# A chunked scan on one core: the solve of its 16x16 blocks on POOL, the scaling of its state on ACT

## The chip, the core and the metric

The kernel runs on one core of one Trainium2 chip. A core has five engines that each take their own queue of instructions in order: PE (matmuls), DVE (VectorE), ACT (ScalarE), POOL (GpSimd) and SP, which here only issues DMAs. They wait for each other through semaphores. The metric is the device time of one execution in microseconds (us), lower is better.

## The reference, cut to what matters

The program is two transformer blocks, one after the other. The first has two layers with a convolution branch and a recurrent branch, the second attention, retention and a mixture of experts. The change touches the recurrence of the first block alone. For each of 8 heads and both directions it is a state of 64x64 that every token updates:

```python
def step(s, inp):
    r_t, k_t, v_t, w_t, kk_t, b_t = inp
    sa = -jnp.einsum("bhvk,bhk->bhv", s, kk_t)
    s = (s * w_t[:, :, None, :] + sa[..., None] * b_t[:, :, None, :]
         + v_t[..., None] * k_t[:, :, None, :])
    y = jnp.einsum("bhvk,bhk->bhv", s, r_t) if emit else None
    return s, y
```

It runs over 256 context tokens and then, from the state they leave, over 512 tokens, forwards and backwards, in each of two layers. Around it stand projections (w_in, w_out, the feed-forward weights), norms and the convolution.

## The kernel before, in words

The scan works in chunks of 64 tokens. Within a chunk the recurrence becomes matrix products and the inverse of a triangular 64x64 matrix; across chunks only the state M (128 partitions, two heads of 64, by 64) is carried.

One call of `scan` is one layer. It has 12 steps: 4 pairs of heads times 3 groups of 256 tokens, and each step takes both directions side by side, four chunks each. Per step:

- `decay` (L843 and on) makes the decays of the group: two matmuls `pz` (L849), tanh and exponentials on ACT, a running sum on DVE (L866). POOL clears four columns of its tile tA first (L860).
- `products` makes the scaled keys on DVE (L886 to L892) and the products `pg` on PE (L904), which DVE masks into GM (L908, or L911 where no output is wanted). `PC` holds the decay up to the end of each chunk.
- `solve` inverts the 16x16 blocks on the diagonal. The blocks lie across partitions in the wrong way, so GM's part is stored to the DRAM tile `nsc` (four stores, L682), loaded back as `NB`, 64 blocks on 64 partitions (L684), solved there, stored to `xsc` (L694), and loaded as X and its transpose by `solved` (four loads, L702). NB has one buffer. The solve itself is a loop over k from 1 to 14 with one product (L689) and one sum (L690) per k, of k(15-k) elements per partition, each of which needs the result of the one before, and one write of ones to the diagonal (L693).
- `inverse` puts the blocks together to 64x64: transposes on DVE (L948, L978), matmuls `py` and `pw` on PE (L954, L963, L984, L993), copies on ACT (L957, L987, L1001) and DVE.
- `chunks` then goes through four chunks, each a chain: psR on PE (L1021, L1024), rg on DVE (L1027), psS on PE (L1031), Z on ACT (L1033), psM on PE (L1039), and the new M on DVE (L1044). L1043 multiplies the old M by PC beforehand, for L1044 to add. Outputs `pyo` (L1051, L1054) are collected beside it.

`scan` interleaves them: while the chunks of step s run, `to_come` brings the inverse of step s+1 and the products, the solve and the decays of later steps, and `others` brings what is left of the convolution (taps on DVE, L533, in steps 0 to 5), modulation weights (matmuls `pada`, layer 0) and the output norms. Before step 0 there is a run-up in which the decays and products of the first three steps, the first two solves and the first inverse are made.

The order of each engine's queue isn't the order of the code. A list scheduler places the traced instructions by their dependences and its own estimates of how long each takes; so a change of engine moves other instructions too. In each queue the result is then taken strictly in order.

Of the kernel before, what the change touches and what calls it, by code (L numbers as in the profile page):

```python
# [16 lines left out]
AF = mybir.ActivationFunctionType  # L17
OP = mybir.AluOpType
# [110 lines left out]
def tile_two_blocks(ctx: ExitStack, tc: tile.TileContext, I: dict, out: bass.AP, dump=None, stop=None):  # L129
    nc = tc.nc  # L130
# [24 lines left out]
    def mmps(shape=None, name="mm"):  # L155
        return bank("mm", shape, name)
# [25 lines left out]
    ones = const.tile([128, 128], F32, name="ones")  # L182
# [491 lines left out]
    def solve(s, T, gs):  # L674

        for q, (d, _) in zip(T, gs):
            src = q["NT"]
            if d:
                src = wk.tile([128, 4, 64], F32, name="Nt", tag="ar", bufs=1)
                nc.vector.transpose(src, q["NT"])  # L680
            for h in range(2):
                nc.sync.dma_start(own(NSC[s % 2], d, h), src[HR[h]])  # L682
        NB = wk.tile([64, 16, 16], F32, name="NB", tag="nb", bufs=1)
        nc.sync.dma_start(NB, blocks(NSC[s % 2]))  # L684
        yield
        for k in range(1, 15):
            t = wk.tile([64, 64], F32, name="nbt", tag="nbt", bufs=1)[:, 0:k * (15 - k)].rearrange("p (a b) -> p a b", a=k)
            sh = [64, k, 15 - k]
            nc.vector.tensor_tensor(t, NB[:, 0:k, k:k + 1].to_broadcast(sh), NB[:, k:k + 1, k + 1:16].to_broadcast(sh), op=OP.mult)  # L689
            nc.vector.tensor_tensor(NB[:, 0:k, k + 1:16], NB[:, 0:k, k + 1:16], t, op=OP.add)  # L690
            if k % 2:
                yield
        nc.vector.tensor_scalar(NB.rearrange("p a b -> p (a b)")[:, 0:256:17], ones[0:64, 0:16], 1.0, None, op0=OP.mult)  # L693
        nc.sync.dma_start(blocks(XSC[s % 2]), NB)  # L694
        yield

# [312 lines left out]
    def chunks(l, S, pr, gs, T, state, emit, final, get):  # L1009
# [4 lines left out]
        def chunk(q, d, n):  # L1014
            po = py[:, d] if emit else None
            c = n if d == 0 else 3 - n
            KR, GM, Z, BT, XI, PC = (q[k] for k in ("KR", "GM", "Z", "BT", "XI", "PC"))
            M = state[d]
            pr_ = bank("sm", None, "psR")
            for h in range(2):  # L1020
                nc.tensor.matmul(pr_[HR[h], 0:64], lhsT=GM[HR[h], 0, c, 0], rhs=Z[0][HR[h], c], start=True, stop=M is None)  # L1021
            for h in range(2):
                if M is not None:
                    nc.tensor.matmul(pr_[HR[h], 0:64], lhsT=KR[HR[h], 0, CS_[c]], rhs=M[HR[h], 0], start=False, stop=True)  # L1024
            yield
            rg = wk.tile([128, 64], F32, name="rg", tag="rg", bufs=2)
            nc.vector.tensor_scalar(rg, pr_[:, 0:64], -1.0, None, op0=OP.mult)  # L1027
            yield
            ps_ = bank("sm", None, "psS")
            for h in range(2):  # L1030
                nc.tensor.matmul(ps_[HR[h], 0:64], lhsT=XI[HR[h], c], rhs=rg[HR[h]], start=True, stop=True)  # L1031
            yield
            nc.scalar.activation(Z[1][:, c], ps_[:, 0:64], AF.Copy)  # L1033
            yield
            if not (final and n == 3):
                pm = bank("sm", None, "psM")
                for i in range(2):
                    for h in range(2):
                        nc.tensor.matmul(pm[HR[h], 0:64], lhsT=BT[HR[h], c, i], rhs=Z[i][HR[h], c], start=i == 0, stop=i == 1)  # L1039
                yield  # L1040
                Mn = get("Mn").rearrange("p (a v) -> p a v", a=2)
                if M is not None:
                    nc.gpsimd.tensor_scalar(M[:, 1], M[:, 0], PC[:, c:c + 1], None, op0=OP.mult)  # L1043
                    nc.vector.scalar_tensor_tensor(Mn[:, 0], pm[:, 0:64], PC[:, c:c + 1], M[:, 1], op0=OP.mult, op1=OP.add)  # L1044
                else:
                    nc.vector.tensor_scalar(Mn[:, 0], pm[:, 0:64], PC[:, c:c + 1], None, op0=OP.mult)
                state[d] = Mn
            if emit:
                if M is not None:
                    for h in range(2):  # L1050
                        nc.tensor.matmul(po[HR[h], c], lhsT=M[HR[h], 0], rhs=KR[HR[h], 1, CS_[c]], start=True, stop=False)  # L1051
                for i in range(2):
                    for h in range(2):
                        nc.tensor.matmul(po[HR[h], c], lhsT=Z[i][HR[h], c], rhs=GM[HR[h], i, c, 1], start=M is None and i == 0, stop=i == 1)  # L1054

        for n in range(4):
            yield from abreast(chunk(q, d, n) for q, (d, g) in zip(T, gs))
# [300 lines left out]
    for t in range(6):  # L1358
        p = bank("pre", None, "rvt")
# [63 lines left out]
    for t in range(4):  # L1423
        for a, n in SEG:
            p = bank("pre", None, "pq")
# [8 lines left out]
    p = bank("w", None, "ppe")  # L1434
# [9 lines left out]
    for t in range(6):  # L1444
        r = LAT[:, 4 + t:5 + t]
        for i in range(2):
            p = bank("pre", None, "pkv")
# [19 lines left out]
    for t in range(6):  # L1467
        rk = SS[:, 4 + t]
        k, kp = KTL[t], KP[:, t:t + 1]
# [241 lines left out]
    for t in range(4):  # L1711
        xr = XR[t // 2][:, t % 2]
        for c in range(2):
            p = mmps(name="prow")
# [502 lines left out]
```

## Time and profile before

| | |
|---|---|
| median of 3 runs | 4015.07 us (4010.14 to 4015.51) |
| profiled execution | 4013.53 us, span 4011.7 us |
| PE, DVE, ACT, POOL busy over the span | 94%, 68%, 42%, 8% |
| scan of layer 0, run-up and steps 0 to 10 | 300 to 676 us |
| scan of layer 1, run-up and steps 0 to 10 | 1525 to 1857 us |

A span is the time from the first to the last instruction. An engine is busy while it has an instruction under way; matmuls are pipelined, so a busy PE isn't PE at its peak. In the rows below a form such as `64x14 f32<-64x14 f32` reads partitions by elements, output from input, and "idle before us" is idle time of the engine just before the group, with what ended it.

### The profile page before, as it was taken

Reading aid. Unit: us, or ns where it says so; the run is one execution under the profiler, and the core shown is the slowest. Engines: PE = TensorE matmul, PEld = TensorE weight load, DVE = VectorE, ACT = ScalarE, POOL = GpSimd, SP = SyncE. Lnnn points to the kernel's source line nnn. Section 1 sums busy time; section 2 is a strip of 40 time slices with the busy share of each in tenths; the row PEclk is TensorE's granted clock in tenths of the full one; section 3 lists DMA queues with packets and bytes.
Section 4 is the critical chain, followed back from the end, with each engine's and each line's share of the span. In section 5 each row is a group of like instructions: output and inputs, shape, how many; then the busy total and the mean of one; then the engine's idle time right before and its main releaser. Section 6 shows DMA issues by size and latency. Waiting matters only on the chain. (4 is left out here: it accounts for less than half of the span.)

```text
span 4011.7 us, 69029 instructions
## 1 busy us (share of the span) xinstructions
PE 3774.9 (94%) x27579; PEld 2827.9 (70%) x27579; DVE 2731.7 (68%) x5439; ACT 1695.0 (42%) x2530; POOL 333.9 (8%) x349
## 2 busy tenths in 40 slices
PE   6998999999999998999999998996999999999997
PEld 4787777888888786776787786675565777664443
DVE  4779865843433778876744545657877899987776
ACT  3233342321212334452322334544655677666555
POOL 0001111000000001110000000001101122122111
PEclk7999999999999998899999998997999999999999
DMA  6122323332322321124445421035979899998996
GB/s 204 47 79 69 115 71 98 117 123 84 126 84 85 100 72 25 32 45 125 152 151 153 106 74 42 1 117 198 360 279 351 306 363 363 371 354 331 374 368 240
DMA packets 353911, 677.75 MB, mean 169 GB/s; under 512 B 118759, under 2 KB 230194, under 8 KB 323474
## 3 DMA queue, kind: packets, MB, share of 16 engines
q1 hardware_dynamic: 343024, 636.89, 45.3%
q0 software_dynamic: 9312, 34.56, 3.4%
q8 instruction: 218, 3.57, 0.4%
q10 hardware_dynamic: 1250, 1.85, 0.1%
q14 instruction: 107, 0.88, 0.1%
HBM read 635.33 MB, written 37.90 MB: 168 GB/s over the span
## 5 line engine op out<-in xcount | busy, mean ns | idle before, releaser
L431 ACT ACTIVATE wh<-wst 128x1024 fp32r<-128x1024 f32 (+2 forms) x222 | 222.7, 1004 | 990.7 <-PE pc L441 513.1
L1830 DVE TENSOR_TENSOR ml<-E,mh 128x2048 fp32r<-128x2048 f32 x236 | 536.2, 2286 | 91.5 <-PE pu L1878 44.3
L1829 ACT ACTIVATE mh<-E 128x2048 fp32r<-128x2048 f32 x236 | 447.6, 1916 | 185.9 <-PE pu L1878 146.8
L441 PE MATMUL px<-Hh,wl 128*128 128x512 f32 (+2 forms) x1216 | 487.8, 402 | 13.8 <-DVE wl L432 13.8
L441 PE MATMUL px<-Hh,wh 128*128 128x512 f32 (+3 forms) x1216 | 486.1, 401 | 13.3 <-ACT wh L431 7.1
L441 PE MATMUL px<-Hl,wh 128*128 128x512 f32 (+3 forms) x1216 | 485.5, 400 | 0.6 <-DVE Hl L419 0.6
L432 DVE TENSOR_TENSOR wl<-wst,wh 128x1024 fp32r<-128x1024 f32 (+2 forms) x222 | 255.4, 1151 | 270.6 <-ACT wh L431 268.4
L1878 PE MATMUL pu<-ml,ch 128*64 128x512 f32 (+2 forms) x968 | 272.3, 399 | 22.4 <-DVE ml L1830 22.2
L1878 PE MATMUL pu<-mh,ch 128*128 128x512 f32 (+1 forms) x968 | 279.3, 403 | 6.9 <-DVE ch L1866 4.2
L441 PEld LDWEIGHTS px<-Hh,wh 128*128 128x128 f32 (+1 forms) x1216 | 232.2, 191 | 72.6 <-ACT wh L431 9.4
L441 PEld LDWEIGHTS px<-Hh,wl 128*128 128x128 f32 (+1 forms) x1216 | 231.8, 191 | 72.8 <-DVE wl L432 18.7
L441 PEld LDWEIGHTS px<-Hl,wh 128*128 128x128 f32 (+1 forms) x1216 | 232.4, 191 | 55.6 <-DVE Hl L419 3.5
L533 DVE SCALAR_TENSOR_TENSOR acc<-ZC,VT,acc 128x272 f32<-128x272 f32 (+2 forms) x600 | 253.0, 477 | 2.5 <-ACT acc L528 2.5
L1878 PEld LDWEIGHTS pu<-mh,ch 128*128 128x128 f32 (+1 forms) x968 | 171.8, 184 | 86.5 <-issue 25.0
L1830 DVE TENSOR_TENSOR ml<-st,mh 128x2048 fp32r<-128x2048 f32 x86 | 196.0, 2286 | 42.8 <-PE pu L1878 24.5
L1878 PEld LDWEIGHTS pu<-ml,ch 128*64 128x64 f32 (+2 forms) x968 | 149.4, 159 | 92.0 <-DVE ml L1830 34.1
L441 PE MATMUL pc<-Hh,wh 128*128 128x256 f32 x672 | 193.0, 288 | 1.0 <-ACT Hh L418 0.9
L441 PE MATMUL pc<-Hl,wh 128*128 128x256 f32 x672 | 191.9, 286 | 0.5 <-DVE Hl L419 0.5
L441 PE MATMUL pc<-Hh,wl 128*128 128x256 f32 (+1 forms) x672 | 190.3, 284 | 0.1
L1829 ACT ACTIVATE mh<-st 128x2048 fp32r<-128x2048 f32 x86 | 163.2, 1917 | 55.3 <-PE pu L1878 31.7
L315 DVE SCALAR_TENSOR_TENSOR as<-adt,CS,as 128x512 f32<-128x512 f32 x224 | 161.3, 747 | 36.4 <-DMA adt<-in_w_ada_dram 20.4
L1134 DVE SCALAR_TENSOR_TENSOR XT<-px,MOD,XT 128x512 f32<-128x512 f32 x66 | 49.4, 749 | 188.0 <-PE px L441 187.7
(602 smaller groups left out, 7864.2 us busy)
## 6 DMA issues: line engine op xcount, KB each, us to landing
E<-in_w_mlp_dram SPq DMA_DIRECT2D x288, 1024.0 KB
st<-in_w_mlp_dram SPq DMA_DIRECT2D x94, 1024.0 KB
wst<-in_w_in_dram SPq DMA_DIRECT2D x29, 1024.0 KB
adt<-in_ada_w_dram SPq DMA_DIRECT2D x96, 256.0 KB
adt<-in_w_ada_dram SPq DMA_DIRECT2D x96, 256.0 KB
wst<-in_ffn_wg_dram SPq DMA_DIRECT2D x22, 1024.0 KB
wst<-in_ffn_wu_dram SPq DMA_DIRECT2D x22, 1024.0 KB
adaw<-in_ada_w_dram SPq DMA_DIRECT2D x16, 1024.0 KB
```

Source lines behind the costliest of these rows:

```text
L315: nc.vector.scalar_tensor_tensor(acc[s], t, c, acc[s], op0=OP.mult, op1=OP.add)
L431: nc.scalar.activation(wh, t[:, :, c0:c0 + n], AF.Copy)
L432: nc.vector.tensor_tensor(wl, t[:, :, c0:c0 + n], f32(wh), op=OP.subtract)
L441: nc.tensor.matmul(p[0:m, 0:n], lhsT=wa[:, k, 0:m], rhs=ha[:, k, a:a + n], start=k == 0 and first, stop=k == nk - 1 and last)
L533: nc.vector.scalar_tensor_tensor(o, z[:, j + a:j + a + n], cw(j), o, op0=OP.mult, op1=OP.add)
L1134: nc.vector.scalar_tensor_tensor(o, src, gate, o, op0=OP.mult, op1=OP.add)
L1829: nc.scalar.activation(wh, t, AF.Copy)
L1830: nc.vector.tensor_tensor(wl, t, f32(wh), op=OP.subtract)
L1878: nc.tensor.matmul(p[0:xa.shape[2]], lhsT=xa[:, kt], rhs=w[part][:, c:c + 512], start=kt == 0 and j == 0, stop=last and j == len(parts) - 1)
```

## The change

Two edits. The solve's products, sums and its write of the diagonal are issued on POOL (`nc.gpsimd`) in place of DVE. The scaling of M by the decay up to the end of the chunk, which stood on POOL, becomes an ACT copy with a scale per partition.

```diff
         for k in range(1, 15):
...
-            nc.vector.tensor_tensor(t, NB[:, 0:k, k:k + 1].to_broadcast(sh), NB[:, k:k + 1, k + 1:16].to_broadcast(sh), op=OP.mult)
-            nc.vector.tensor_tensor(NB[:, 0:k, k + 1:16], NB[:, 0:k, k + 1:16], t, op=OP.add)
+            nc.gpsimd.tensor_tensor(t, NB[:, 0:k, k:k + 1].to_broadcast(sh), NB[:, k:k + 1, k + 1:16].to_broadcast(sh), op=OP.mult)
+            nc.gpsimd.tensor_tensor(NB[:, 0:k, k + 1:16], NB[:, 0:k, k + 1:16], t, op=OP.add)
             if k % 2:
                 yield
-        nc.vector.tensor_scalar(NB.rearrange("p a b -> p (a b)")[:, 0:256:17], ones[0:64, 0:16], 1.0, None, op0=OP.mult)
+        nc.gpsimd.tensor_scalar(NB.rearrange("p a b -> p (a b)")[:, 0:256:17], ones[0:64, 0:16], 1.0, None, op0=OP.mult)
...
                 if M is not None:
-                    nc.gpsimd.tensor_scalar(M[:, 1], M[:, 0], PC[:, c:c + 1], None, op0=OP.mult)
+                    nc.scalar.activation(M[:, 1], M[:, 0], AF.Copy, scale=PC[:, c:c + 1])
                     nc.vector.scalar_tensor_tensor(Mn[:, 0], pm[:, 0:64], PC[:, c:c + 1], M[:, 1], op0=OP.mult, op1=OP.add)
```

The scheduler then orders all queues anew. Three places show it. In the names, `nsc_258` and `nsc_259` (`xsc_260` and `xsc_261`) are the two DRAM tiles, used in turn by even and odd steps; `XT`, `scanbuf` are the large tiles from which the scan cuts its buffers.

SP, the DMA queue, in the first steps of layer 1's scan, before:

```order
L684 DMA NB<-nsc_259 64x16x16
L682 DMA nsc_258<-scanbuf_14542 64x4x64 x2
L682 DMA nsc_258<-Nt 64x4x64 x2
L694 DMA xsc_261<-NB 64x16x16
L702 DMA XT<-xsc_261 64x4x64 x4
L684 DMA NB<-nsc_258 64x16x16
```

The same place in the change:

```order
L684 DMA NB<-nsc_259 64x16x16
L694 DMA xsc_261<-NB 64x16x16
L702 DMA XT<-xsc_261 64x4x64 x4
L682 DMA nsc_258<-scanbuf_14542 64x4x64 x2
L682 DMA nsc_258<-Nt 64x4x64 x2
L684 DMA NB<-nsc_258 64x16x16
```

The stores of the next step's blocks to nsc, which stood between the load of NB and the store of its result, now stand behind the loads of that result.

PE, layer 1, where the inverse for step 3 stands, before:

```order
L1021 MATMUL psR<-scanbuf_14543,scanbuf_14542 64x64 x4
L954 MATMUL py<-XT,scanbuf_14542 64x64 x16
L963 MATMUL pw<-XT 64x64 x16
L904 MATMUL pg<-scanbuf_14543,XT 64x128 x9
L984 MATMUL py<-XT,scanbuf_14542 64x32 x16
L904 MATMUL pg<-scanbuf_14543,XT 64x128
L993 MATMUL pw<-XT 32x32 x16
L924 MATMUL pt<-CF,XT 64x64 x32
```

And in the change:

```order
L1031 MATMUL psS<-rg,XT 64x64 x2
L1051 MATMUL pyo<-scanbuf_14543,XT 64x64
L904 MATMUL pg<-scanbuf_14543,XT 64x128 x7
L954 MATMUL py<-XT,scanbuf_14542 64x64 x16
L904 MATMUL pg<-scanbuf_14543,XT 64x128 x9
L1031 MATMUL psS<-rg,XT 64x64 x2
L963 MATMUL pw<-XT 64x64 x16
L1039 MATMUL psM<-scanbuf_14543 64x64 x8
```

The inverse stood in one piece between the last chunk of step 2 and the first of step 3; now its first matmuls stand among the second chunk of step 2, beside the products pg of step 4.

POOL, the run-up of layer 0 (an ISA row sets the engine up for the operation behind it), before:

```order
L652 MEMSET scanbuf_2187 128x1032
L860 MEMSET tA 128x4 x6
L1043 ISA
L1043 TENSOR_SCALAR XT<-XT,PC 128x64 x8
L860 MEMSET tA 128x4 x2
```

And in the change:

```order
L652 MEMSET scanbuf_2187 128x1032
L860 MEMSET tA 128x4 x2
L689 ISA
L689 TENSOR_TENSOR nbt<-NB 64x14
L693 TENSOR_SCALAR NB<-ones 64x16
L690 TENSOR_TENSOR NB<-NB,nbt 64x14
L860 MEMSET tA 128x4
L689 TENSOR_TENSOR nbt<-NB 64x26
```

The solve has taken the place of the scaling of M, and the clearing of tA for the decays stands among its operations.

## Rows read from the trace of the kernel before

**Rows 1.** The page's first part: busy us, share of the span, instructions.

```profile
PE 3774.9 (94%) x27579; PEld 2827.9 (70%) x27579; DVE 2731.7 (68%) x5439; ACT 1695.0 (42%) x2530; POOL 333.9 (8%) x349
```

**Rows 2.** Busy time by stage: stretch, its length, busy us (instructions), clock, DMA share, GB/s.

```profile
core 0: us, PE busy (x) PEld busy (x) DVE busy (x) ACT busy (x) POOL busy (x), PEclk, DMA share, GB/s
300.00:345.00 45.00, 34.84 (x536) 28.78 (x532) 43.00 (x138) 20.11 (x49) 0.42 (x4) 0.84 0.16 30
345.00:527.00 182.00, 172.34 (x3328) 134.21 (x3330) 149.00 (x556) 73.52 (x192) 26.48 (x53) 0.97 0.40 116
527.00:676.00 149.00, 140.60 (x2644) 111.04 (x2646) 100.73 (x369) 54.94 (x144) 19.31 (x45) 0.98 0.22 53
1525.00:1568.00 43.00, 33.39 (x539) 27.02 (x539) 34.69 (x119) 20.67 (x50) 0.62 (x6) 0.83 0.17 31
1568.00:1727.00 159.00, 147.46 (x2997) 123.45 (x2999) 130.11 (x501) 72.64 (x191) 25.69 (x54) 0.88 0.16 32
1727.00:1857.00 130.00, 120.68 (x2347) 93.42 (x2344) 87.47 (x330) 49.42 (x136) 18.34 (x42) 0.96 0.24 56
```

**Rows 3.** The solve's products and sums: count, ns min/median/max, first and last start.

```profile
L689 DVE TENSOR_TENSOR nbt<-NB x336: 123/190/264, 313.3 to 1836.1; 64x14 f32<-64x14 f32 x24, 64x36 f32<-64x36 f32 x24, 64x50 f32<-64x50 f32 x24, 64x56 f32<-64x56 f32 x24
...
L690 DVE TENSOR_TENSOR NB<-NB,nbt x336: 134/187/271, 313.5 to 1836.3; 64x14 f32<-64x14 f32 x24, 64x36 f32<-64x36 f32 x24, 64x50 f32<-64x50 f32 x24, 64x56 f32<-64x56 f32 x24
```

**Rows 4.** Timeline of SP's queue, start of layer 1's scan: start us, us, issue.

```profile
1555.19 0.57 SPq L684 DMA_DIRECT2D NB<-nsc  x1
1555.81 1.34 SPq L682 DMA_DIRECT2D nsc<-scanbuf  x2
1557.19 1.27 SPq L682 DMA_DIRECT2D nsc<-Nt  x2
1570.23 0.57 SPq L694 DMA_DIRECT2D xsc<-NB  x1
1574.18 2.58 SPq L702 DMA_DIRECT2D XT<-xsc  x4
1576.87 0.57 SPq L684 DMA_DIRECT2D NB<-nsc  x1
```

**Rows 5.** The same queue in the run-up of layer 0's scan.

```profile
306.31 1.24 SPq L682 DMA_DIRECT2D nsc<-Nt  x2
309.19 0.60 SPq L684 DMA_DIRECT2D NB<-nsc  x1
...
328.21 0.57 SPq L694 DMA_DIRECT2D xsc<-NB  x1
```

**Rows 6.** M's scaling on POOL: all; then layer 0's steps 0-5, 6-10.

```profile
L1043 POOL TENSOR_SCALAR XT<-XT,PC x160: 434/446/2484, 347.3 to 1864.2; 128x64 f32<-128x64 f32 x160
...
L1043 POOL TENSOR_SCALAR XT<-XT,PC 128x64 f32<-128x64 f32 x40 | 24.4, 618 | 124.7 <-DVE XT L1044 61.2 <-DVE NB L690 57.1 <-DVE nbt L689 6.2
...
L1043 POOL TENSOR_SCALAR XT<-XT,PC 128x64 f32<-128x64 f32 x36 | 16.5, 468 | 97.6 <-DVE XT L1044 71.7 <-DVE nbt L689 11.6 <-DVE XT L1046 10.1
```

**Rows 7.** Timeline of POOL from 465.3 to 469.2 us.

```profile
466.17 3.04 POOL L1043 TENSOR_SCALAR XT<-XT,PC 128x64 f32<-128x64 f32 x2 [13.03 <-DVE NB L690]
```

**Rows 8.** Timeline of DVE in the same stretch, two of 18 rows.

```profile
466.40 0.41 DVE L886 TENSOR_TENSOR scanbuf<-zz,tB 128x256 f32<-128x256 f32 x1
466.73 0.18 DVE L690 TENSOR_TENSOR NB<-NB,nbt 64x36 f32<-64x36 f32 x1
```

**Rows 9.** Other operations on POOL: ns min/median/max, starts; second, a sum of two inputs.

```profile
L173 POOL CAST CM<-cmf x1: 292/292/292, 5.7 to 5.7; 128x128 int8<-128x128 f32 x1
...
L1791 POOL TENSOR_TENSOR hr<-hr,AS x8: 1257/1378/3041, 2730.9 to 2748.5; 128x512 f32<-128x512 f32 x8
L1791 POOLq EVENT_SEMAPHORE  x7: 17/43/43, 2730.3 to 2743.8; - x7
```

**Rows 10.** ACT by line and shape, 345 to 527 us: busy us, mean ns, idle before.

```profile
L1033 ACT ACTIVATE scanbuf<-psS 128x64 f32<-128x64 f32 x48 | 9.4, 224 | 37.2 <-PE psS L1031 37.2
...
L885 ACT ACTIVATE tA<-tA,KC,VT 128x256 f32<-128x256 f32 x10 | 6.0, 596 | 3.2 <-DVE tA L866 3.2
```

## The prediction

> **What bounds the kernel now.** I read the page's busy table first, then busy time by stage, then the rounds of the solve on the DMA queue. Over the whole span PE is busy 94% of the time and DVE 68% [rows 1], but the edit touches the two scans alone, and there the picture is another one. Six stages matter [rows 2]: for layer 0 the run-up (300 to 345 us), steps 0 to 5 (345 to 527) and steps 6 to 10 (527 to 676), for layer 1 the run-up (1525 to 1568), steps 0 to 5 (1568 to 1727) and steps 6 to 10 (1727 to 1857). In the four stages with steps PE lacks work for 9.7, 8.4, 11.5 and 9.3 us, 38.9 us in all: that is all that any relief of DVE could give back there. A step lasts 182/6 = 30.3 us, 149/5 = 29.8, 159/6 = 26.5 and 130/5 = 26.0 us.
>
> Beside PE runs a second thing that repeats in every step, the round of the solve. The queue of SP loads NB, waits for the solve, stores it to xsc, loads X from there, and only then loads the next NB, since NB has one buffer. In layer 1 this reads: NB issued at 1555.19, store at 1570.23, loads of X from 1574.18, next NB at 1576.87 [rows 4], a round of 21.7 us, of which 15.0 lie between load and store and 6.7 after it. The store of the next step's blocks to nsc (1555.81 to 1558.46) lies inside the round, under the solve, and costs it nothing. A round of 21.7 us fits into a step of 26 us.
>
> **The change, part by part.** *DVE loses the solve*: 336 products (L689) and 336 sums (L690) of 0.19 us each [rows 3], some 127 us of records over 24 solves. DVE is busy 149 of 182 us in layer 0's steps 0 to 5 [rows 2]; its queue gets shorter, and whatever PE waits for from DVE comes earlier. The gain lies between nothing (PE has enough to do anyway) and the 38.9 us of PE's idle time. Where the round, below, sets the step, nothing is gained, and that is layer 1's steps 0 to 5; of the other three stages (27.4 us idle) I take about half, since ACT and DMA end waits of PE too: **-13 us**.
>
> *POOL gets the solve.* No row of before shows a two-input operation of 14 to 56 elements on POOL. The nearest are these. A one-input conversion of 128 elements takes 0.292 us and a two-input one of 512 elements 1.257 us at least [rows 9]. The 28 operations have 40 elements on average (the sum of k(15-k) over 14 values of k is 560), so they read 80, fewer than the 128 of the first row; an estimate a little under it is 0.27 us. The scaling of M, with 64 elements and a scalar per partition, took 0.446 us in the median [rows 6]. Each of the 28 waits for the one before it; handling a wait took 0.04 us on this queue [rows 9]. So one operation costs between 0.31 and 0.49 us; I take 0.38, nearer to the low end, since the solve's operations have no scalar operand but broadcast and strided ones.
>
> To that comes the port. The same scaling of M took 0.618 us on average in layer 0's steps 0 to 5 and 0.468 in steps 6 to 10, against its median of 0.446 and a worst case of 2.484 us [rows 6]. The worst one shows why: the pair at 466.17 us needed 3.04 us [rows 7] while DVE ran one operation with two inputs in SBUF after the other, at their usual 0.18 and 0.41 us [rows 8]. POOL stood still and DVE did not. [...] So I add 0.17 us per operation in steps 0 to 5, where the convolution's taps run on DVE, and 0.02 later (0.618 and 0.468 less 0.446): a solve of 28 x 0.55 + 0.4 = 15.8 us early and 28 x 0.40 + 0.4 = 11.6 us late, the 0.4 for the diagonal. [...]
>
> *The queue of SP is written in another order.* Behind the run-up, the order of the changed program has the stores to nsc of the next step after the loads of X, not before the store to xsc. They come out of the solve's shadow into the round: 2.6 us to issue [rows 4] and 1.6 us from the last store to the NB load that needs it (307.55 to 309.19, [rows 5]). From the NB load to the first product are 4.1 us (309.19 in [rows 5], 313.3 in [rows 3]). The round is then 4.1 + solve + 6.7 + 2.6 + 1.6 = **15.0 us + solve**: 30.8 us early, 26.6 late. Layer 0: 30.8 against steps of 30.3 is 0.5 x 6 = 3 us, and late 26.6 against 29.8 nothing. Layer 1: 30.8 against 26.5 is 4.3 x 6 = 26 us, and late 26.6 against 26.0, for four steps that have a solve, 2 us. Sum: **+31 us**. Queued behind the waiting xsc store on SP are those nsc stores, the loads of X and layer 0's ada weights; PE waits for them at L954.
>
> *PE's order follows suit.* Counted over the order, 1.34 steps of psS matmuls lie between a step's last pg and its first py in before (mean of steps 3 to 11 of both layers), 0.91 in the change. PE takes its queue in order, so at L954 it stands where the round is late. This is the place at which the 31 us are paid; it isn't counted twice.
>
> *The run-up.* The first solve took 19.0 us from load to store (309.19 to 328.21, [rows 5]); on POOL 4.1 + 15.8 = 19.9, and more if the taps hold the port, in both layers. Bounds 0 and 16 us (twice the 7.8 us by which a starved solve, below, is longer); I take **+4**.
>
> *M's scaling goes to ACT*: 160 operations. A copy of 64 elements from PSUM took 0.224 us there, one of 256 elements from SBUF with two operands per partition 0.596 [rows 10]; I take 0.35, 56 us in all on an engine busy 73.5 of 182 us [rows 2]. The scaled M is wanted only after psR, rg, psS, Z and psM of the next chunk, which hides it; behind it in ACT's queue wait the copies of Z and py. Bounds 0 and 56 us, taken **+2**; without that move it would have stood behind the solve on POOL.
>
> Sum: -13 + 31 + 4 + 2 = **+24 us** on the profiled execution's 4013.5 us (4011.7 us of span and 1.8 around it). That run lies 1.5 us under the median of the runs, so the forecast in terms of the median is 4039 us.
>
> **The rivals.** *Faster*: POOL is quick enough. At 0.31 us and no port waits a solve takes 9.1 us, the round 24.1 us, under every stage's step; the 31 us vanish and DVE's relief stays, up to 36 us of the 38.9: 3980 at best, about 3992 as a middle. It decides at a round of 26.5 us, a solve of 11.5 us or 0.40 us per operation with its waits. For it speaks that POOL is empty in the scans; against it the 0.618 us of early scalings. *Nothing to measure*: the round just fits, and PE's own work hides the rest: 4015. *Starved*: at 0.49 us and twice the port wait early solves take 28 x 0.83 + 0.4 = 23.6 us, late ones 15.2; rounds of 38.6 and 30.2 cost 50 + 73 + 2 + 17 = 142 us and the run-up 16: 4170 at the end, 4110 as a middle. For it speaks the one 2.48 us row, against it that such rows are few: the median is 0.446.
>
> **How the numbers follow.** The forecast (8 to 60 us slower) 0.42; faster 0.30; no difference 0.16; starved 0.12. A difference of 0.2%, 8 us, is about what a measurement of this kernel can tell from none. Slower is 0.54, same 0.16, faster 0.30. The range leaves out the far half of the starved case and the tail of the faster one: 3980 to 4100, reaching over the low bound of POOL's cost to much of the high one.
>
> **What would show it.** L689 and L690 on POOL with spacings near 0.4 us late and 0.55 early; 15 to 16 us from first product to diagonal in early steps; nsc stores on SP behind the loads of X; steps of layer 1's first half near 30 us, with PE idle before py at L954; layer 0's second half a little shorter. If the spacing is under 0.40 us early too, or steps of layer 1 don't grow although the round does, the forecast is wrong; if solves take over 20 us, it is too low.

## The result, and the profile after

The change makes the kernel slower: 4122.1 us (median of 4 runs, 4108.9 to 4127.3) against 4015.3 us for the kernel before on the same chip (4 runs, 4010.1 to 4018.5), a ratio of 1.027 with a 95% interval of 1.0245 to 1.0295. That is 107 us more, where the forecast had 24 and the range ended at 4100. The direction was right, the size was not, and neither was the mechanism, as the rows show.

First the page's busy table of the kernel after (its span is 4106.9 us), to be held against [rows 1]:

```profile
PE 3781.5 (92%) x27579; PEld 2846.9 (69%) x27579; DVE 2660.9 (65%) x4743; ACT 1738.0 (42%) x2689; POOL 468.5 (11%) x885
```

DVE has lost 696 instructions and 71 us of busy time (2731.7 less 2660.9), POOL has gained 135, ACT 43. The work has moved as the diff says, and no engine is near its limit through it. The stages, cut at the same events as in [rows 2] (the stages with steps run from the first Z of a scan to that of its step 6 and on to that of its step 11), columns as there:

```profile
300.00:342.00 42.00, 26.94 (x474) 23.75 (x471) 32.20 (x80) 15.05 (x37) 16.19 (x51) 0.77 0.15 25
342.00:556.00 214.00, 181.05 (x3417) 143.93 (x3414) 141.89 (x400) 91.00 (x244) 61.31 (x197) 0.92 0.35 100
556.00:722.00 166.00, 143.43 (x2616) 114.20 (x2616) 84.33 (x232) 64.41 (x179) 38.44 (x128) 0.93 0.20 48
1570.00:1612.00 42.00, 29.59 (x484) 24.89 (x486) 21.29 (x54) 15.39 (x38) 14.76 (x54) 0.69 0.15 26
1612.00:1793.00 181.00, 145.42 (x3012) 123.67 (x3008) 115.84 (x327) 78.91 (x229) 60.63 (x193) 0.88 0.15 29
1793.00:1956.00 163.00, 130.23 (x2384) 104.52 (x2384) 77.71 (x220) 66.53 (x184) 37.20 (x127) 0.84 0.18 44
```

The four stages with steps now last 214 + 166 + 181 + 163 = 724 us, against 182 + 149 + 159 + 130 = 620 in [rows 2]: 104 us, the whole loss (the two profiled spans differ by 95 us). PE lacks work in them for 33.0 + 22.6 + 35.6 + 32.8 = 124 us, against 38.9. So 85 of the 104 us are new idle time of PE. The other 19 are PE being busy longer with about the same matmuls (11429 records against 11316): its granted clock is 0.92, 0.93, 0.88 and 0.84 in place of 0.97, 0.98, 0.88 and 0.96. Each of these values is a mean of time at the full clock (1.0) and time at half of it (0.5), the only two values in both traces; the matmuls of pyo (L1054) average 219 ns at the one and 311 at the other in the kernel after. The run-ups are no longer than before: the first Z comes at 342.1 us against 345.5 in layer 0, and in layer 1 890 us after the first Z of layer 0's last step, against 892.

What PE waits for, from the table of waits of the kernel before, and then of the kernel after (us in total, times, longest):

```profile
PE py L954 <- DVE XT L948: 7.6, 7, 2.4
```

```profile
PE py L954 <- DVE XT L948: 98.0, 18, 10.4
```

This one wait, the first matmul of the inverse for the transposed X, has grown by 90 us. Two of the 18 waits, 20 us, lie in the run-ups, which did not become longer; the other 16, 78 us, lie in the 22 steps, in all four stages (14.4, 11.9, 28.1 and 23.4 us). They make up most of the 85 us. It is not POOL that is slow. The solve's operations on POOL, grouped by line (count, busy us and mean ns, idle before):

```profile
L690 POOL TENSOR_TENSOR NB<-NB,nbt 64x14 f32<-64x14 f32 (+6 forms) x336 | 107.8, 321 | 24.3
L689 POOL TENSOR_TENSOR nbt<-NB 64x14 f32<-64x14 f32 (+6 forms) x336 | 106.9, 318 | 350.9 <-DMA NB<-nsc 326.6
```

POOL idles for the load of NB, and for nothing else of note. From the first product to the last operation a solve takes 11.3 us on average (9.4 to 12.9 over 24 solves, worked out from their starts and ends), where DVE had needed 13.3 with other work in between. The solve has become shorter, and X comes later. How, the queues show around one step of layer 1. First SP, to be held against [rows 4]:

```profile
1657.07 0.59 SPq L684 DMA_DIRECT2D NB<-nsc  x1
1672.41 0.57 SPq L694 DMA_DIRECT2D xsc<-NB  x1
1674.96 2.61 SPq L702 DMA_DIRECT2D XT<-xsc  x4
1677.61 1.27 SPq L682 DMA_DIRECT2D nsc<-scanbuf  x2
1683.55 1.24 SPq L682 DMA_DIRECT2D nsc<-Nt  x2
1686.51 0.59 SPq L684 DMA_DIRECT2D NB<-nsc  x1
```

Then PE in the same stretch (in brackets the idle time before an instruction and what ended it):

```profile
1672.96 1.08 PE L904 MATMUL pg<-scanbuf,XT 64*64 64x128 f32 x14
1678.62 1.97 PE L954 MATMUL py<-XT,scanbuf 64*64 64x64 f32 x32 [4.57 <-DVE XT L948]
1680.38 1.51 PE L904 MATMUL pg<-scanbuf,XT 64*64 64x128 f32 x16
```

And DVE:

```profile
1678.12 0.45 DVE L948 STREAM_TRANSPOSE XT<-XT 128x256 f32<-128x256 f32 x1 [4.49 <-DMA XT<-xsc]
...
1681.06 0.69 DVE L908 TENSOR_TENSOR scanbuf<-pg,CB 128x512 f32<-128x512 f32 x1 [0.85 <-PE pg L904]
...
1682.15 0.69 DVE L908 TENSOR_TENSOR scanbuf<-pg,CB 128x512 f32<-128x512 f32 x1
```

Read it as one chain: the solve ends and is stored (1672.41), X is loaded (1674.96), transposed on DVE (1678.12), used by py on PE (1678.62). Only then come the last nine of the 32 products pg of the *next* step (1680.38; one matmul of the program makes two records here). They need nothing of X; they merely stand behind py in PE's queue. Then their masks (1681.06 to 1682.8), the store of the last of them (1683.55), the load of NB (1686.51), and the next solve. From one load of NB to the next are 29.4 us, against 23.3 in the same place of the kernel before (21.7 two rounds earlier, in [rows 4]). Between store and next load lie 14.1 us (1672.41 to 1686.51), where the prediction had 10.9. In the kernel before the products of step s+2 stand ahead of the py of step s+1 in 18 of the 20 places of the two scans, so they wait in no such chain. After the change they stand behind it, wholly (11 places) or in part (7), in 18 of 20. Mean step length is (380 + 344)/22 = 32.9 us against (331 + 288)/22 = 28.1, from the starts of the first Z of each step; 4.8 us in each of 22 steps.

### The profile page after: what moved, and what is told of

It reads as the page before. It is cut to its first block, busy times and chain, and to the rows that moved or that the text cites. A ratio compares the mean times of both kernels' runs of the same rounds, so it can differ in the third digit from the quotient of the medians.

```text
span 4106.9 us, 68998 instructions
## 1 busy us (share of the span) xinstructions
PE 3781.5 (92%) x27579; PEld 2846.9 (69%) x27579; DVE 2660.9 (65%) x4743; ACT 1738.0 (42%) x2689; POOL 468.5 (11%) x885
## 5 line engine op out<-in xcount | busy, mean ns | idle before, releaser
L441 PE MATMUL px<-Hh,wl 128*128 128x512 f32 (+2 forms) x1216 | 484.5, 399 | 13.3 <-DVE wl L432 13.3
L1957 POOL DMA_INDIRECT out_dram<-XT,idx x34 | 117.0, 3441 | 512.8 <-DVE XT L1955 284.5
```

The lines of the kernel that those rows point to most:

```text
L441: nc.tensor.matmul(p[0:m, 0:n], lhsT=wa[:, k, 0:m], rhs=ha[:, k, a:a + n], start=k == 0 and first, stop=k == nk - 1 and last)
L1957: nc.gpsimd.indirect_dma_start(out=ov, out_offset=bass.IndirectOffsetOnAxis(ap=idx[:, 0:1], axis=0), in_=y, in_offset=None, compute_op=OP.add)
```

## Experiments

The theory from here on, the **order theory**: the loss is not the price of the solve on POOL, but of the order in which the scheduler, given the new engine, put products and inverse on PE, DVE and SP. Its rivals: POOL itself (how long its operations take, and how long they wait beside DVE), and the scaling of M on ACT. Each ratio below is against runs of the kernel before on the same chip. Not all rows are of one chip: the kernel before has medians of 4013.7 to 4015.8 us beside them, so that differences between rows are good to about 2 us at best. The last column is the wait at py for the transposed X in the profiled run.

| kernel | median us | ratio, 95% interval | wait at py, us |
|---|---|---|---|
| after | 4122.1 | 1.0270 (1.0245 to 1.0295) | 98.0 |
| e1_solve_only | 4140.6 | 1.0304 (1.0271 to 1.0338) | 105.1 |
| e2_m_only | 4017.5 | 1.0011 (0.9993 to 1.0028) | 8.7 |
| e4_before_py_first | 4156.1 | 1.0351 (1.0326 to 1.0376) | 55.7 |
| e5_order_back | 4021.7 | 1.0021 (1.0009 to 1.0034) | 21.6 |
| e6_pe_dve_back | 4052.3 | 1.0091 (1.0074 to 1.0108) | 36.7 |
| e7_after_half | 4028.2 | 1.0038 (1.0027 to 1.0050) | 29.1 |
| e7_after_double | 4210.7 | 1.0484 (1.0461 to 1.0506) | 153.5 |
| e8_back_double | 4083.9 | 1.0168 (1.0151 to 1.0185) | 23.5 |
| e9_runup | 4043.3 | 1.0072 (1.0055 to 1.0089) | 1.9 |
| e10_runup_xsc | 4037.1 | 1.0064 (1.0044 to 1.0083) | 0.2 |
| e11_xsc | 4028.8 | 1.0033 (1.0019 to 1.0047) | 23.0 |
| e12_runup_dve | 4027.6 | 1.0034 (1.0022 to 1.0045) | 2.9 |
| e13_runup_pool | 4028.8 | 1.0033 (1.0020 to 1.0046) | 0.2 |
| e14_runup_dve | 4022.0 | 1.0015 (1.0003 to 1.0027) | 0.7 |
| e15_before_sp | 4034.3 | 1.0044 (1.0027 to 1.0061) | 5.8 |

### Each part of the change alone

e1 is the kernel after with the scaling of M back on POOL (the edit shown), e2 the kernel before with the opposite edit:

```diff
-nc.scalar.activation(M[:, 1], M[:, 0], AF.Copy, scale=PC[:, c:c + 1])
+nc.gpsimd.tensor_scalar(M[:, 1], M[:, 0], PC[:, c:c + 1], None, op0=OP.mult)
```

> The solve stands on POOL as in the kernel after, the scaling of M stays on POOL as in the kernel before. Order theory (the solve's move changed the order in which PE, DVE and SP take the products of step s+2 and the inverse of step s+1, and that order costs the 107 us): the order on PE is almost that of the kernel after, so 4105 to 4135 us, about 4120. Rival, the scaling on ACT carries a part of the loss (it stands in the chunk chain): below 4100, down to 4030 if it carries most. Rival, the two POOL streams collide now that the 88 scalings of a layer share POOL with the solve: above 4135.

> The scaling of M stands on ACT, the solve stays on DVE. Order theory: the order of products and inverse stays that of the kernel before, so within 8 us of it, 4007 to 4023 us. Rival, the scaling on ACT lengthens the chunk chain by its wait in ACT's queue: 4035 to 4100 us.

Measured: 4140.6 and 4017.5 us. The whole loss comes with the solve; the scaling on ACT alone makes no difference that can be measured. e1 lies above the band of the order theory and in that of the third expectation, of two POOL streams that collide. But its interval overlaps that of the kernel after, so neither such a collision nor a gain from the scaling's move beside the solve on POOL is shown.

### The order of the kernel after, made on the kernel before

Solve and scaling stay on DVE and POOL, as in the kernel before. The one edit is a pin of issue order on PE (no wait, only the place in the queue); the scheduler orders the other queues after it:

```diff
+    m = nc.tensor.matmul(pg[HR[h], c, 0:nt], lhsT=BK[HR[h], c, i], ...)
+    if i and LEFT:          # LEFT: last py matmul of the step traced before
+        behind(m, LEFT[0])
```

> The kernel before, with solve and scaling where they were, but each product matmul of step s+2 is queued on PE behind the first inverse matmul (py) of step s+1, as the kernel after has it. Order theory: products, stores, solve, loads and inverse become one round per step, of about 35 us from the last mask to the inverse (22 without the solve plus 13 of solve) and 5 us from py to the next mask, 40 us against steps of 28 us: slower than before by 100 to 250 us, 4115 to 4265. Rival, the loss of the kernel after is a matter of POOL (its latency or its port): the solve is on DVE here, so 4010 to 4040 us.

Measured: 4156.1 us, 141 above the kernel before. The kernel before can be made as slow as the kernel after, and slower, without the solve on POOL. In all 20 places three quarters or more of the products now stand behind py. SP's queue then shows the same serial round, 33.1 us from one load of NB to the next, with the stores in two parts behind the loads of X:

```profile
1704.04 0.59 SPq L684 DMA_DIRECT2D NB<-nsc  x1
1719.91 0.57 SPq L694 DMA_DIRECT2D xsc<-NB  x1
1722.46 2.61 SPq L702 DMA_DIRECT2D XT<-xsc  x4
1730.79 1.25 SPq L682 DMA_DIRECT2D nsc<-scanbuf  x2
1734.15 1.23 SPq L682 DMA_DIRECT2D nsc<-Nt  x2
1737.11 0.59 SPq L684 DMA_DIRECT2D NB<-nsc  x1
```

The wait at py itself is 55.7 us here, less than in the kernel after; part of the time is waited elsewhere (19.3 us at pg, for the DVE product that writes its operand, against 11.6 in the kernel before). So the wait at py is the sign of the round, not its measure.

### The order of the kernel before, with the change in

e5 keeps solve on POOL and scaling on ACT. In the program the inverse of step s+1 is written behind the products and stores of step s+2, and three pins hold it there:

```diff
-                for _ in range(3):
+                for _ in range(2):
                     yield next(works[0])
             if s + 2 < 12:
                 works.append(blocks_then_decays(s + 2))
+                for _ in range(3 + ((s + 2) % 3 == 0)):
+                    yield next(works[1])
...
-            solved(s, Ts[s], parts(s)[2], get)
             yield from every(transposed, s)
+            solved(s, Ts[s], parts(s)[2], get)
...
+    behind(<load of X>, "SP"), behind(<transpose of X>, "DVE"), behind(<py matmul>, "PE")
```

> The kernel after, solve on POOL and scaling on ACT, but the inverse of step s+1 is written behind the products and the stores of step s+2 and pinned there on PE, DVE and SP (its loads of X behind the stores, its transposes behind the masks, py behind the products), which is nearly the order of the kernel before on PE. Order theory: at least two thirds of the 107 us come back, 3985 to 4050 us, about 4010, and PE's waits at py fall from about 99 us to under 30. Rival, POOL's solve itself or the scaling on ACT is what costs: 4090 to 4130 us.

Measured: 4021.7 us. Of the 107 us 100 have come back, with every operation on the engine on which the change put it. The wait at py is 21.6 us, nearly all of it two waits in the run-ups. SP's queue in layer 1:

```profile
1654.75 1.21 SPq L690 DMA_DIRECT2D NB<-nsc  x1
1656.01 0.67 SPq L708 DMA_DIRECT2D XT<-xsc  x1
1669.05 0.59 SPq L700 DMA_DIRECT2D xsc<-NB  x1
1682.12 1.25 SPq L688 DMA_DIRECT2D nsc<-scanbuf  x2
```

The solve is over at 1669.05 and SP waits 13 us for the next products: here the round has slack, and PE's work sets the step. This is the most of any early step of layer 1. In this order the stores to nsc of the next step stand behind the store of the solved blocks, which isn't the order of the kernel before ([rows 4]), and in 5 of the 22 places of the two scans SP issues them within 0.1 us of it: there the round has no slack left. The same shows at py in layer 1's steps 0 to 5, first in the kernel after, then in e5 (count, busy us, mean ns, idle before):

```profile
L954 PE MATMUL py<-XT,scanbuf 64*64 64x64 f32 x192 | 13.2, 306 | 28.1 <-DVE XT L948 28.1
```

```profile
L962 PE MATMUL py<-XT,scanbuf 64*64 64x64 f32 x192 | 10.3, 245 | 0.1
```

The remaining 7 us above the kernel before are near the limit of what can be told, and where they lie isn't settled.

### Which queue: SP alone

e6 is e5 with the loads of X of step s+1 ahead of the stores of step s+2 on SP, as the kernel after has them; e15 is the kernel before with that order on SP and no other edit.

```diff
+    m = nc.sync.dma_start(own(NSC[s % 2], d, h), src[HR[h]])
+    if LOADS:               # LOADS: last load of X traced before
+        behind(m, LOADS[0])
```

> As e5_order_back, with PE and DVE pinned to the order of the kernel before, but SP keeps the order of the kernel after throughout: the stores of step s+2 are queued behind the loads of X of step s+1. This is the round that the prediction on record counted (about 15 us of queue and transfers plus the solve), with the solve at the 11 us that the traces show: 26 us, under the steps of 28 us of the kernel before. If the loss sits in the order on PE and DVE: 4005 to 4045 us. If the order on SP carries a third of it or more: 4055 to 4110 us.

> The kernel before with SP alone in the order of the kernel after: the stores of the products of step s+2 are queued behind the loads of X of step s+1. PE and DVE keep products ahead of inverse. The prediction's round then is 15.0 us plus the solve's 13.3 on DVE, 28.3 us a step against 28 to 30: 4020 to 4055 us. If the order on SP costs nothing by itself: 4008 to 4022. If it costs as much as the order on PE: 4110 to 4160.

Measured: e6 4052.3 us, between the two bands, 31 above e5 (28 by the ratios, since the two ran on different chips); e15 4034.3, inside the band of the round, 19 above the kernel before. So the order on SP has a price of its own, 19 to 31 us of the 107. The round in e15:

```profile
1614.54 0.57 SPq L698 DMA_DIRECT2D xsc<-NB  x1
1618.13 2.60 SPq L706 DMA_DIRECT2D XT<-xsc  x4
1620.78 1.28 SPq L684 DMA_DIRECT2D nsc<-scanbuf  x2
1622.10 1.28 SPq L684 DMA_DIRECT2D nsc<-Nt  x2
1625.08 0.59 SPq L688 DMA_DIRECT2D NB<-nsc  x1
1642.74 0.57 SPq L698 DMA_DIRECT2D xsc<-NB  x1
```

10.5 us from store to load of NB, 28.2 from store to store: in this step the prediction's 10.9, and its round of 15.0 us + the solve, as it was worked out. It is the round of *this* kernel, not of the kernel after. The 19 us don't lie where the prediction's sum has them, though: the steps of layer 0 grew by 8 us and those of layer 1 by 12, where a round of 28.3 us would cost nothing in layer 0.

### The solve made shorter and longer

e7_after_half cuts the loop over k to 1 to 7 in the kernel after and so leaves half of the solve out; the two doubled kernels issue the product of each stage twice, in the kernel after and in e5.

```diff
-        for k in range(1, 15):
+        for k in range(1, 8):
```

```diff
             nc.gpsimd.tensor_tensor(t, NB[:, 0:k, k:k + 1].to_broadcast(sh), ..., op=OP.mult)
+            nc.gpsimd.tensor_tensor(t, NB[:, 0:k, k:k + 1].to_broadcast(sh), ..., op=OP.mult)
```

> The kernel after with the elimination of the 16x16 blocks cut to its first 7 of 14 stages (this part of the computation is left out), 15 POOL instructions for 29; products and inverse still stand on PE as in the kernel after. Order theory: the solve is a link of one serial round per step, so its 5.4 us (14 instructions by about 0.39) come off each of some 20 steps until PE is the bound: up to 108 us less, 4015 to 4060. Rival, the loss is a fixed cost of the order, the solve itself is not in it: 4095 to 4125 us.

> The kernel after with each of the 14 multiplications of the solve done twice (43 POOL instructions for 29), order on PE as in the kernel after. Order theory: 5.4 us more in each of some 20 rounds, 4190 to 4240 us, about 4230. Rival, the solve is not in the round: 4120 to 4145 us.

> e5_order_back with each of the 14 multiplications of the solve done twice. Order theory: with products and stores of step s+2 ahead of the inverse of step s+1 the solve has slack (the inverse of e5_order_back starts 14.8 us after the solve's end on average), so the 5.4 us are mostly hidden: 4015 to 4050 us. Rival, the solve's length counts in any order: 4090 to 4130 us.

The solves, from starts and ends, last 5.9 us halved, 11.3 as they are, 16.3 doubled in the kernel after (16.1 in e8). The times are 4028.2, 4122.1 and 4210.7 us: 94 us for 5.4 us of solve, 88 us for 5.0. Both are about 17.5 us per us, as if the solve were a link of the serial round in 17 or 18 of the 24 steps (an estimate). Both times lie in the bands of the order theory, which supports the mechanism from another side. It isn't a proof by itself: the scheduler ordered these two kernels anew (products wholly ahead of py in 1 of the 20 places in the halved, in 5 in the doubled, in 2 in the kernel after).

e8 is a miss: 4083.9 us, 62 above e5, where 0 to 30 were expected; it lies between the two bands, nearer to the rival's. 12 us per us of solve remain in the better order. By stage, e5 and then e8 (the steps of layer 0 cut at the first Z of step 5, those of layer 1 at that of step 6):

```profile
343.00:497.00 154.00, 144.47 (x2827) 113.83 (x2825) 121.30 (x345) 71.20 (x200) 50.81 (x169) 0.99 0.38 104
497.00:685.00 188.00, 176.58 (x3203) 137.87 (x3201) 102.73 (x286) 84.17 (x222) 47.08 (x155) 0.96 0.27 70
1575.00:1726.00 151.00, 142.83 (x3026) 119.71 (x3022) 119.18 (x337) 83.12 (x234) 58.39 (x198) 0.93 0.18 35
1726.00:1864.00 138.00, 123.87 (x2365) 97.31 (x2364) 74.14 (x209) 62.85 (x176) 34.75 (x122) 0.94 0.22 51
```

```profile
345.00:518.00 173.00, 154.38 (x2839) 123.83 (x2837) 122.21 (x345) 72.39 (x201) 72.05 (x246) 0.92 0.32 93
518.00:711.00 193.00, 176.51 (x3197) 137.99 (x3191) 103.13 (x285) 84.08 (x222) 66.63 (x230) 0.96 0.27 69
1610.00:1776.00 166.00, 149.76 (x3022) 125.29 (x3020) 120.28 (x337) 84.58 (x237) 83.60 (x276) 0.90 0.16 32
1776.00:1920.00 144.00, 127.51 (x2364) 100.84 (x2362) 73.83 (x208) 62.24 (x174) 53.64 (x192) 0.91 0.21 49
```

The early parts have grown by 19 and 15 us, the late ones by 5 and 6 (the first late one, 188 to 193, by 5.4 in its last step alone); the rest of the 62 us lies in the run-ups and behind the scans. The mean slack of 14.8 us between a solve's end and its inverse, on which the expectation rested, hides that some early steps have far less. In e5 steps 0, 1 and 3 of layer 0 have 5.7, 7.6 and 8.4 us, steps 0 and 1 of layer 1 5.6 and 9.0, and 5.5 us is the shortest way from the end of a solve on POOL through SP to DVE's transpose among the 24 solves of the kernel after. And the round through SP is still there: the next stores stand behind the store of the solved blocks. In e8 they follow it within 0.3 us in 10 of 22 places, where e5 has 5, as here:

```profile
1640.95 0.59 SPq L701 DMA_DIRECT2D xsc<-NB  x1
1641.59 2.23 SPq L688 DMA_DIRECT2D nsc<-scanbuf  x2
```

The next store of solved blocks comes at 1668.55, 27.6 us later, in layer 1, whose early steps took 25.2 us in e5 (151/6). A longer solve is paid at once there.

### Does the move pay at equal order on PE?

e13 is e5 with the run-up in the order of the kernel before too (products of step 2 ahead of the first inverse); e14 is e13 with the solve back on DVE, scaling on ACT included. Products and py on PE, masks and transposes on DVE stand in the same order in both (but for one matmul). SP's queue doesn't: in e14 some stores to nsc stand ahead of the store of the solved blocks that in e13 stand behind it, in the run-ups and in several early steps.

```diff
...
-        run(inverse_of(0))
+        first_inverse = inverse_of(0)
+        for _ in range(2):
+            next(first_inverse)
         run(blocks_of(1))
         run(decays(2))
+        ahead[2] = blocks_then_decays(2)
+        for _ in range(2):
+            next(ahead[2])
+        run(first_inverse)
```

> e5_order_back with the products of step 2 ahead of the first inverse in the run-up, as in e9_runup, but with the transposes of step 0 still ahead of those products, so that nothing is overwritten that step 0 reads. If the 15 us by which e9_runup was slower than its twin with the solve on DVE came from there: 4005 to 4022 us. If they come from the solve on POOL behind this order on SP: 4030 to 4045 us.

> e13_runup_pool with the solve back on DVE, the order of products, masks and inverse the same on PE and DVE. If the solve on POOL is worth its 13 us of DVE relief at equal order: 8 to 25 us above e13_runup_pool. If DVE's load is hidden beside PE: within 6 us of it. If POOL is the worse place even at equal order: 8 to 20 us below it. As to the kernel before, about 4015 to 4030 us.

Measured: 4028.8 us on POOL, between the two bands of its expectation, and 4022.0 on DVE, 7 below, between the bands too. The intervals overlap; what they exclude is the gain of 8 us or more for POOL. The steps of layer 0 and of layer 1 in e13, and then in e14 (stretches, columns as above):

```profile
351.00:685.00 334.00, 315.21 (x5981) 247.68 (x5975) 217.19 (x617) 149.75 (x409) 92.78 (x304) 0.97 0.31 86
1588.00:1872.00 284.00, 262.81 (x5337) 215.06 (x5334) 187.18 (x534) 141.11 (x399) 90.31 (x306) 0.92 0.19 41
```

```profile
345.00:683.00 338.00, 320.72 (x5977) 250.80 (x5975) 248.70 (x912) 150.31 (x409) 4.79 (x22) 0.96 0.32 86
1578.00:1859.00 281.00, 257.88 (x5334) 207.46 (x5333) 215.35 (x825) 140.62 (x397) 3.69 (x20) 0.96 0.20 43
```

DVE is relieved of 31.5 + 28.2 = 60 us of busy time, and the steps take 618 us with POOL and 619 with DVE. With PE busy for 92 to 95% of them either way, DVE's load is hidden. The run-ups favour the kernel with the solve on DVE: the first Z of layer 0 comes at 345 us against 352, that of layer 1 895 us after layer 0's last step against 903. How much of that is the engine and how much SP's order isn't separated. What follows the scans evens it out in the profiled pair (spans of 4025.0 us in e13 and 4026.9 in e14), so that a difference either way is not shown. The run-up's new order did not help e5 either: the 20 us of waits at py are gone, the first Z comes later instead (352 us in layer 0 against 343 in e5).

### Variants that gave nothing

Four kernels looked for a version that beats both. In e9, e10 and e12 the products of step 2 stand ahead of all of step 0's inverse in the run-up, its transposes included; BK has buffers for two steps, so those transposes read operands of step 2, which changes that part of the computation. e10 and e11 also issue the store of the solved blocks on POOL:

```diff
-        nc.sync.dma_start(blocks(XSC[s % 2]), NB)
+        nc.gpsimd.dma_start(blocks(XSC[s % 2]), NB)
```

> e5_order_back, and in the run-up of each layer's scan the products of step 2 stand ahead of the first inverse too, as in the kernel before. In e5_order_back PE waits there at py for X, 10.8 us in layer 0 and 10.1 in layer 1, in the kernel before under 0.2. Order theory: some of these 21 us come back, at most 20: 4002 to 4018 us, about 4010. Rival, the waits only move to the next link of the run-up: 4018 to 4030 us.

> e9_runup with the store of the solved blocks issued by POOL, behind the solve, in place of SP: on SP nothing of step s+2 waits any more for the solve of step s+1. If a round through SP still binds in some steps (e8_back_double lost 62 us to 5 us more of solve): 3990 to 4010 us. If PE's own work is the bound by now: as e9_runup within 6 us. If a store issued by POOL comes later than one by SP: 5 to 30 us above e9_runup.

> e5_order_back with the store of the solved blocks issued by POOL, without the change to the run-up. If the round through SP still binds: 4000 to 4016 us. If PE is the bound: 4016 to 4028. If the store by POOL comes later: 4030 to 4050.

> e9_runup with the solve back on DVE: the same order of products, inverse and stores on PE and DVE, only the engine of the solve differs. If taking 149 us of solve off DVE is worth the 13 us of the prediction, and the shorter solve on POOL (11.0 against 13.3 us) something more: 10 to 40 us above e9_runup. If PE hides both: within 6 us of e9_runup.

Measured: 4043.3, 4037.1, 4028.8 and 4027.6 us, none under the kernel before and none of the gains expected; e9 and e12 lie outside all their bands. Of e9 and e12, the overwritten forms of e13 and e14, the one with the solve on POOL is 16 us slower than the one on DVE, and their intervals don't overlap. They too differ in SP's order in the first steps. Why e9 is 14 us above e13 was not followed up. The store on POOL brings nothing that can be measured (e10 against e9 and e11 against e5: intervals overlap), which fits the slack that SP has in most places of e5. No run found a version faster than the kernel before.

## Why the prediction was wrong

**The step that failed** is the one on PE's order: "This is the place at which the 31 us are paid; it isn't counted twice." It took py's earlier place in PE's queue for a mere place of waiting, set by the round on SP. But what stands behind py there is pg of the next step, the start of the next round. With that the round is no longer SP's alone: X, transpose, py, pg, mask, store, NB, solve, X, one link after the other. The excerpt of PE's order ahead of the prediction shows it, py between 7 and 9 matmuls of pg; the prediction counted the mean distance (1.34 to 0.91 steps) and didn't ask who waits behind. e4 makes the loss by one pin of that order on PE, which the other queues follow; e5 takes it away by order alone, with every engine as the change has it. Of the 107 us about 70 are the order on PE and DVE (4122.1 to 4052.3 of e6), about 30 that on SP (e6 to e5), 7 are left in e5. The shares hold for this way back; made on the kernel before, SP's order alone costs 19 us (e15).

That PE takes its queue in order shows in the trace: the nine products that needed nothing of X came only when py had gone, behind 4.57 us of waiting in the rows above.

**The round on SP, +31 us.** That e6 lost 28 to 31 us by this order is luck as to the number, for two errors stand in the sum. The solve was taken at 15.8 us early; it took 11.3 (11.5 and 11.3 in the early steps of the two layers). With 11.3 the round is 26.3 us, and the same sum gives about 1 us (0.3 us in each of four late steps of layer 1). What e6 lost lies in both layers, about 8 us in the steps of layer 0 and 24 in those of layer 1; by which wait is not shown. And the round was taken to end with the stores, with their data ready. In the kernel after the last of them waits for the last masks (1683.55, 5.9 us behind the first).

**The solve on POOL.** 0.38 us per operation, waits included, was right for the spacing (11.3 us less 0.4 by 28 is 0.39), though the operation alone came at 0.28 in the median and 0.32 in the mean, not at the 0.34 that 0.38 less 0.04 for the wait makes. The 0.17 us that it added in early steps, its port wait, was wrong: L689 takes 322 ns on average in layer 0's first half and 305 in its second. The pair at 466.17 us [rows 7] made only part of it: without its operation of 2.484 us the 40 early scalings still averaged 0.57 us against the median of 0.446 of all [rows 6]. That the scaling takes longer beside DVE holds over all 160, by starts and ends: the 62 with no DVE operation of two inputs in SBUF beside them took 0.434 to 0.452 us, the other 98 took 0.60 us on average and up to 2.48, of them 25 beside taps alone 0.54. "Port" is the prediction's name for this; the traces show the longer times beside DVE and nothing behind them. What failed was to carry the size of that stretching over to the solve's operations, of which no row stood there. They stretch too, but little on the whole. The longest product on POOL took 1.68 us from 312.64 us, while DVE ran four operations with two inputs in SBUF without a break until 314.24. Over all 672 the mean lies only 0.04 us above the median.

**DVE's relief, -13 us**, didn't come: nothing to measure at equal order on PE (e13 against e14). The load taken off was overstated besides. 672 records of 0.19 us are 127 us, but DVE's busy time fell by 71. In the kernel before only 56 us of the solve's records had no other DVE record beside them: records overlap on one engine, so that a sum of durations isn't the time set free.

**The run-up, +4 us**: the first Z came 3 us earlier in layer 0 (345.5 to 342.1) and the run-up of layer 1 was 2 us shorter. **Scaling on ACT, +2 us**: nothing to measure (e2), and 347 ns each in the median where 350 was taken; the row that answers to [rows 6] (count, ns min/median/max, starts):

```profile
L1043 ACT ACTIVATE XT<-XT,PC x160: 331/347/359, 343.2 to 1964.6; 128x64 f32<-128x64 f32 x160
```

**The rivals.** "Faster" was to decide at a solve of 11.5 us. The solve came in under that, and the kernel still got slower by four times the forecast: the condition was on the wrong quantity. "Starved" had the time, 4110, by a mechanism that didn't happen. A rival that was never named is the one that held: that the new order puts the next round's start behind this round's end. Of the list of what would show it, the nsc stores behind the loads of X, PE's idle time before py and the steps near 30 us in layer 1's first half (181/6 = 30.2) came true, the solves of 15 to 16 us and the shorter second half of layer 0 (166 us against 149) did not. A spacing under 0.40 us in early steps, which the prediction had named as a sign against itself, came too. With PE waiting before py in all four stages, the cause that was offered, a long early solve, could not be it.

## What to carry to other kernels

Where a scheduler sets the order, moving one step to another engine moves others with it: look in the new order for an instruction that waits on a long chain, and ask which instructions behind it in the same queue start the next pass of that chain. If there are any, the pass is serial, and its length is the sum of all links, not that of the slowest queue. Relief of an engine is worth only what the bound engine waits for it: with PE busy for about 93% of the steps, 60 us less on DVE brought nothing that could be measured. And a cheap trial tells order from cost: pin the old order with the new engines, and the new order with the old ones.

## What the runs showed of the hardware

Small two-input operations on POOL (64 partitions, 14 to 56 elements, f32) take 0.20 to 0.38 us for most, 0.28 in the median, and follow one another at 0.39 us when each needs the one before. Such a chain ran faster on POOL (11.3 us) than on a shared DVE (13.3 us), although DVE needs 0.19 us for one, because of what stood in between: on DVE 9 to 33 other instructions in each solve, on POOL none in 21 of the 24 and two at the most:

```profile
1661.18 0.23 POOL L690 TENSOR_TENSOR NB<-NB,nbt 64x26 f32<-64x26 f32 x1
1661.48 0.52 POOL L689 TENSOR_TENSOR nbt<-NB 64x36 f32<-64x36 f32 x1
1662.08 0.37 POOL L690 TENSOR_TENSOR NB<-NB,nbt 64x36 f32<-64x36 f32 x1
1662.53 0.33 POOL L689 TENSOR_TENSOR nbt<-NB 64x44 f32<-64x44 f32 x1
```

Single operations stretch (0.52 us here, 1.68 at the most over 672), and they do so beside DVE: the 386 with no DVE operation of two inputs in SBUF beside them took 0.25 us on average (all but one under 0.30), the other 286 took 0.41, and the twelve longest are all among these. This is what the traces show together; no run varied it alone. DVE's own operations of that kind became a little longer in the scans (L892: 409 to 466 ns on average).

The second thing is that PE's waits went with more than their length. With 85 us more of idle time the granted clock of three of the four stages fell (0.97, 0.98 and 0.96 to 0.92, 0.93 and 0.84), and up to 19 us of slower matmuls came on top. In all, PE had 65 us at half the clock in the four stages before and 154 after, the rest at the full clock. Idle time alone doesn't tell it: in layer 1's first half it rose from 11.5 to 35.6 us, and the clock stayed at 0.88.
